# Opening of a hybrid decoder layer: norm 1's shift and scale by pairs of feature tiles on VectorE, the opening's order in a table, the causal mask in VectorE's maximum, keys flipped once

## The chip, the cores and the metric

The kernel runs on one core of one Trainium2 chip. The metric is the device time of one execution in microseconds (us). Engines by their names in the profile: PE is TensorE's matmul, PEld its weight load, DVE is VectorE, ACT is ScalarE, POOL is GpSimd, SP is SyncE, which issues nearly all transfers.

## What is computed

One decoder layer on 512 tokens of 1024 features, float32. Reduced to what matters here:

```python
sh1, sc1, gt1, sh2, sc2, gt2 = split(silu(c) @ w_ada + b_ada)      # 6 x 1024
h = rmsnorm(x, norm1_g) * (1.0 + sc1) + sh1
z = h @ w_in                      # HGRN2 q, f, i, g; NSA q; 6 key/value parts; gates
o_hg = hgrn2(hq, hf, hi, hgt, lb, hg_norm_g)        # 4 heads of 128, gated recurrence
q = rope(rmsnorm(nq)); k_c, k_s, k_w = rope(rmsnorm(kc)), ...   # 8 heads of 64, 2 key heads
# three attention branches: compressed keys, selected blocks, window; each a causal softmax
x = x + gt1 * (concat(o_hg, o_nsa) @ w_out)
h2 = rmsnorm(x, norm2_g) * (1.0 + sc2) + sh2
a, v = split(causal_dwconv(h2 @ w_up))
x = x + gt2 * ((silu(a) * v) @ w_down)
```

## The kernel before

Every large product is taken with both factors split into a high part (rounded by a cast) and a low part (the difference): `split` (L139 to L141) casts on ScalarE and subtracts on VectorE, and `mm3` (L143 to L146) does three products of 512 columns, high x high, high x low, low x high. The features are eight tiles of 128 (k = 0 to 7); the tokens are four tiles of 128.

**The opening.** x is loaded, normed and transposed into `xnT` (eight tiles of 128 x 512). For each feature tile k the shift and the scale are `silu(c) @ w_ada` for 2 x 128 columns; their 1 MB of w_ada comes in four transfers of 256 KB (L282, tiles `ada`), whose contiguous runs are 128 floats. The 1024 x 256 product is made in one of two ways. `ada_first_row` (L378) does it on TensorE: 8 products of 256 columns on each of the four row groups, one after another, into `warm`, copied to `row` on ScalarE. It is used for k = 0, 1 and those in `ROWS` (2, 3, 5). `ada_sum` (L392) does it on VectorE for k = 4, 6, 7 (`SUMS`): one multiplication (L401) and seven multiply-and-add steps (L399) of 128 x 256, into `rows`. `ada_col` (L406) turns the row into two columns by two tiny products `adc` (L411). `h_scale` (L414) makes shift and scale from them; `h_tile` (L429) has ScalarE scale the tile (L439) and cast it (L440), and VectorE subtract (L445) for the low part. The loop over k then does 18 products of 512 columns per tile: four token tiles of the NSA queries (`accq`) and two column tiles of the first forget gates (`accf`). The query weights of a tile (`raw`, 256 KB) and the gate weights of two tiles (`rawf`, 256 KB) are split as they come. `COLS` places `ada_col` and `h_tile` of tile k+1 between the products of tile k. GpSimd only makes powers for the norms and the rope tables (L485 to L527) in this part.

**Behind the opening.** A string `ORDER` interleaves generators letter by letter: `d` the dense projections, `p` the preparation of queries and keys, `a` attention, `s` the later sums of w_ada on VectorE (L1333, L1335), `l` and `m` the recurrence. The preparation of one unit (queries q0 to q3; keys k0 to k3; compressed keys a0 to a3) has four steps: `s` squares, `r` the root (GpSimd's power, L357), `n` norm and rope (L693 to L702), `f` the transposes (L751 queries, L797 keys, L838 compressed keys and values). For keys each head's 64 columns are written twice next to each other (`dup` = 2), so that one transpose gives them on partitions 0 to 63 and 64 to 127. In `scores` two key branches are handled together for the first two token tiles (n = 2): the causal mask is added by one more product of 256 columns (`identb` x `causb`, L981), and VectorE takes the maximum (L982). For the last two token tiles (n = 1) VectorE adds the mask `cmask` and takes the maximum in one instruction, with the result read by a second (L978).

Each engine does its instructions in the order in which the program gives them, and waits where an operand isn't ready.

## Time and profile before

| what | value |
|---|---|
| median of three runs | 699.65 us (699.53 to 701.13) |
| the profiled execution | 699.39 us |
| its span | 697.6 us |
| granted TensorE clock, mean | 1.00 |
| bytes moved | 90.16 MB, 129 GB/s over the span |

A row of a timeline gives the start, the length, the engine, the line, the operation, output<-inputs by the program's names, the shape, and how often it is repeated; in brackets stands the idle time ahead of it and what ended it. A row of groups gives busy time and mean nanoseconds of one. A row of waits gives the waiting engine and line, what it waited for, the sum, the times and the longest.

### The profile page before, as it was taken

What the parts mean: (1) busy time and instruction counts of PE and PEld (TensorE: products, weight loads), DVE (VectorE), ACT (ScalarE), POOL (GpSimd) and SP (SyncE); (2) the same over time, 40 slices, a digit from 0 to 9 for tenths busy, and PEclk for the clock granted to TensorE, in tenths of its full rate; (3) what the DMA queues carried; (4) which work ended last, traced back from release to release, by engine and by line L of the source; (5) the groups of instructions that cost most, each with busy time, mean ns of one, the idle gap of its engine ahead of it and who ended that gap; (6) DMA issues with size and microseconds to landing.
All of it is one profiled execution on the core that took longest, in us unless ns stands there. A gap on an engine that the chain in (4) does not pass through costs nothing.

```text
span 697.6 us, 10902 instructions
## 1 busy us (share of the span) xinstructions
PE 687.0 (98%) x4263; PEld 566.5 (81%) x4264; DVE 453.2 (65%) x882; ACT 326.0 (47%) x624; POOL 117.5 (17%) x119
## 2 busy tenths in 40 slices
PE   8999999999999999999999999999999999999997
PEld 4678898787887879888988888888888888888886
DVE  5588989968889879688656666655555554225224
ACT  5564446665676778245444443344433443111210
POOL 2005022200020200100047437511011010000000
PEclk9999999999999999999999999999999999999999
DMA  9996443568213226162053454523424323124301
GB/s 284 295 291 196 124 148 97 187 205 272 92 33 121 62 62 214 59 178 69 12 163 117 132 152 122 150 71 110 121 61 120 96 86 122 62 101 170 120 31 60
DMA packets 100487, 90.16 MB, mean 129 GB/s; under 512 B 5787, under 2 KB 83539, under 8 KB 100437
## 3 DMA queue, kind: packets, MB, share of 16 engines
q1 hardware_dynamic: 100181, 89.38, 42.0%
q8 instruction: 33, 0.54, 0.3%
q10 hardware_dynamic: 256, 0.11, 0.1%
q14 instruction: 17, 0.14, 0.1%
HBM read 87.37 MB, written 2.11 MB: 128 GB/s over the span
## 4 chain that ended last, share of the span: by engine, by line
PE 77%; DVE 10%; ACT 5%; DMA 4%; SPq 2%; issue 1%; POOL 0%; ACTq 0%; DVEq 0%
PE u L146 11%; PE u L144 11%; PE u L145 11%; PE dn L144 6%; PE dn L145 6%; PE dn L146 6%; PE pT L144 2%; PE pT L146 2%; PE pT L145 2%; PE oT L1059 2%; PE F L1031 2%; PE oh L144 2%; PE oh L146 2%; PE oh L145 2%; DMA raw<-in_w_in 1%; DVE rows L399 1%
## 5 line engine op out<-in xcount | busy, mean ns | idle before, releaser
L141 DVE TENSOR_TENSOR wlo<-raw,whi 128x1024 fp32r<-128x1024 f32 (+1 forms) x87 | 111.3, 1280 | 136.1 <-ACT whi L140 135.5
L140 ACT CAST whi<-raw 128x1024 fp32r<-128x1024 f32 (+1 forms) x87 | 89.8, 1032 | 102.3 <-PE dn L146 80.1
L144 PE MATMUL u<-h2h,whi 128*128 128x512 f32 (+1 forms) x360 | 136.7, 380 | 0.0
L145 PE MATMUL u<-h2l,whi 128*128 128x512 f32 (+1 forms) x360 | 136.7, 380 | 0.0
L146 PE MATMUL u<-h2h,wlo 128*128 128x512 f32 (+1 forms) x360 | 136.6, 380 | 0.0
L145 PEld LDWEIGHTS u<-h2l,whi 128*128 128x128 f32 x360 | 67.7, 188 | 12.9
L146 PEld LDWEIGHTS u<-h2h,wlo 128*128 128x128 f32 x360 | 67.7, 188 | 12.8
L144 PEld LDWEIGHTS u<-h2h,whi 128*128 128x128 f32 x360 | 67.7, 188 | 12.7
L145 PE MATMUL dn<-wlo,gT 128*128 128x512 f32 (+1 forms) x160 | 62.1, 388 | 0.0
L146 PE MATMUL dn<-whi,gT 128*128 128x512 f32 (+1 forms) x160 | 62.1, 388 | 0.0
L144 PE MATMUL dn<-whi,gT 128*128 128x512 f32 (+1 forms) x160 | 62.0, 388 | 0.0
L1623 POOL TENSOR_TENSOR y<-y,y 128x512 f32<-128x512 f32 x22 | 28.4, 1290 | 165.7 <-DVE y L1618 165.7
L140 ACT CAST gT<-y 128x512 fp32r<-128x512 f32 x20 | 12.4, 622 | 71.2 <-POOL y L1623 71.2
L141 DVE TENSOR_TENSOR gT<-y,gT 128x512 fp32r<-128x512 f32 x20 | 14.8, 742 | 42.7 <-ACT gT L140 42.7
L144 PE MATMUL pT<-hT,whi 128*128 128x512 f32 x96 | 39.2, 409 | 0.0
L146 PE MATMUL pT<-hT,wlo 128*128 128x512 f32 x96 | 37.7, 393 | 0.0
L145 PE MATMUL pT<-hT,whi 128*128 128x512 f32 x96 | 37.5, 391 | 0.0
L1621 ACT ACTIVATE y<-y 128x512 f32<-128x512 f32 x22 | 13.9, 632 | 49.6 <-DVE y L1618 49.6
L145 PEld LDWEIGHTS dn<-wlo,gT 128*128 128x128 f32 x160 | 30.0, 188 | 6.4 <-DVE wlo L141 0.2
L144 PEld LDWEIGHTS dn<-whi,gT 128*128 128x128 f32 x160 | 30.0, 188 | 6.2
L146 PEld LDWEIGHTS dn<-whi,gT 128*128 128x128 f32 x160 | 30.0, 188 | 6.2
L1616 ACT ACTIVATE y<-u,cv 128x512 f32<-128x512 f32 x44 | 33.9, 772 | 0.0
(378 smaller groups left out, 1410.2 us busy)
## 6 DMA issues: line engine op xcount, KB each, us to landing
raw<-in_w_up SPq DMA_DIRECT2D x44, 512.0 KB, 4.2
aw<-in_w_ada SPq DMA_DIRECT2D x24, 512.0 KB, 4.0
raw<-in_w_down SPq DMA_DIRECT2D x10, 1024.0 KB, 5.1
ada<-in_w_ada SPq DMA_DIRECT2D x32, 256.0 KB, 5.7
raw<-in_w_in SPq DMA_DIRECT2D x7, 1024.0 KB, 6.6
x<-in_x SPq DMA_DIRECT2D x8, 512.0 KB, 4.8
raw<-in_w_cmp SPq DMA_DIRECT2D x8, 512.0 KB, 5.6
raw<-in_w_out SPq DMA_DIRECT2D x4, 1024.0 KB, 6.1
```

The lines of the kernel that those rows point to most:

```text
L140: sc.copy(hi, src)
L141: (eng or ve).tensor_tensor(lo, src, f32(hi), ALU.subtract)
L144: pe.matmul(o, ah, bh, start=start, stop=False, skip_group_check=True)
L145: pe.matmul(o, ah, bl, start=False, stop=False, skip_group_check=True)
L146: pe.matmul(o, al, bh, start=False, stop=stop, skip_group_check=True)
L399: ve.scalar_tensor_tensor(t, w, cs[:, j:j + 1], t, ALU.mult, ALU.add)
L1031: pe.transpose(ps[:, j * P:(j + 1) * P], src[:, j * P:(j + 1) * P], ident)
L1059: pe.matmul(oTs[i][r:r + 64, h // 2], VV[:, j, b, g], src[:, q * P:(q + 1) * P], start=(h == 0 and b == 0 and j == 0), stop=False, skip_gr ...
L1616: sc.activation(y, u, AF.Identity, bias=cv[:, 132 + c:133 + c], scale=cv[:, 88 + c:89 + c])
L1621: sc.activation(y, y, AF.Silu)
L1623: gp.tensor_tensor(ys[0], ys[0], y, ALU.mult)
```

## The change

1. `GROUPS`: the feature tiles are handled as (0,), (1,), (2,3), (4,5), (6,7). Pairs are loaded by 256-column pieces (contiguous runs twice as long, 512 KB in a tile of two), and VectorE sums all three pairs, in 8 steps of 128 x 512 (L605, L607). TensorE makes rows for tiles 0 and 1 only.
2. The opening is written out by the table `OPEN`, one letter a step: `d` loads (their order in `LOADS`), `R` rows, `s` a step of a sum, `c` columns, `h` shift, scale and the high part, `l` or `g` the low part on VectorE or on GpSimd, `w` or `v` the query weights likewise, `f` or `e` the gate weights, `P` a part of the products. Twelve subtractions of 128 x 512 are thereby on GpSimd (4 of h, 5 of query weights, 3 of gate weights). The products of a tile go by kind (high x high for four token tiles, then high x low, then low x high).
3. ScalarE makes high part and scaled tile by two activations in place of an activation and a cast.
4. The rope tables, the first preparation steps and the forget gates are letters of `ORDER`, behind the opening.
5. The mask product is gone; every unit's mask and maximum are VectorE's combined instruction, for n = 2 once for each half.
6. Keys and compressed keys are no longer doubled: half as many transposes. ScalarE and VectorE write the two partition halves, and GpSimd copies one half of the high part (L861). The rope addition (L702) goes to GpSimd (L761).

```diff
-ROWS = (2, 3, 5)
-COLS = (0, 0, 1, 1, 2, 1, 2, 2)
-SUMS = {3: (4, 4, 4), 5: (6, 5, 3), 6: (7, 5, 3)}
-QUICK = 7
+GROUPS = ((0,), (1,), (2, 3), (4, 5), (6, 7))
+LOADS = "aqfaqmaqfqaqfqaqfqci"
+PROWS = (0, 1)
+OPEN = ("cvsshdPsPslRsPPsevPsddsdPsPPchgPdhsdPsdPsvvPgPPePPPsscPhsgPdsPPPhsvgsPssPPesshfPhllcwPPPPwtPP",)
...
     def load_ada():
-        k = len(ada)
+        ks = GROUPS[len(ada)]
+        c, per = len(ks) * P, 4 // len(ks)
         r = []
-        for half in range(2):
-            t = G([4, 2, P], s="ada")
+        for j in range(0, KT, per):
+            t = G([per, 2, c], s="ada")
             for e in range(2):
-                sp.dma_start(t[:, :, e], ada_first[:, 4 * half:4 * half + 4, e, k * P:(k + 1) * P])
-            r.append(t)
+                sp.dma_start(t[:, :, e], ada_first[:, j:j + per, e, ks[0] * P:ks[0] * P + c])
+            r += [t[:, a] for a in range(per)]
...
+    def sums_first():
+        for g in range(len(GROUPS)):
+            if g in PROWS:
+                continue
+            need("a", g + 1)
+            t = TMP([P, 2, len(GROUPS[g]) * P], tag="rows")
+            for j in range(KT):
+                if j:
+                    ve.scalar_tensor_tensor(t, ada[g][j], cs[:, j:j + 1], t, ALU.mult, ALU.add)
+                else:
+                    ve.tensor_scalar(t, ada[g][j], cs[:, 0:1], None, ALU.mult)
+                if j == KT - 1:
+                    arow[g] = t, ones[:, 0:1]
+                yield
...
+            for o in (h[:, 0], xk):
+                sc.activation(o, xk, AF.Identity, bias=sh1[:, k:k + 1], scale=a1[:, k:k + 1])
...
+            (gp if last["l"] == "g" else ve).tensor_tensor(hT[k][:, 1], xnT[k // 2][:, k % 2], f32(hT[k][:, 0]),
+                                                           ALU.subtract)
...
+            qw.append(first_weights(k, gp if last["w"] == "v" else None))
...
+            fw.append(first_gates(k, gp if last["f"] == "e" else None))
...
-            ve.tensor_tensor(dst[:, a, :, :, 0:16], dst[:, a, :, :, 0:16],
+            gp.tensor_tensor(dst[:, a, :, :, 0:16], dst[:, a, :, :, 0:16],
                              rt[:, a].unsqueeze(2).to_broadcast([P, g, dup, 16]), ALU.add)
...
         def flip_k(n):
             ps = PS()
+            for b in range(2):
+                pe.transpose(ps[:, b * P:(b + 1) * P], n[2][:, b].rearrange("p g a e -> p (g a e)"), ident)
+            ends = slice(0, 64), slice(64, 128)
             for g in range(2):
-                for b in range(2):
-                    pe.transpose(ps[:, (2 * g + b) * P:(2 * g + b + 1) * P],
-                                 kd[:, b, g].rearrange("p a e -> p (a e)"), ident)
-            for g in range(2):
-                split(KK[g, 0][:, i], KK[g, 1][:, i],
-                      ps[:, g * 256:g * 256 + 256].rearrange("p (b n) -> p b n", b=2))
+                pv = ps[ends[g], 0:256].rearrange("p (b n) -> p b n", b=2)
+                sc.copy(KK[g, 0][ends[g], i], pv)
+                gp.tensor_copy(KK[g, 0][ends[1 - g], i], KK[g, 0][ends[g], i])
+                for r in range(2):
+                    ve.tensor_tensor(KK[g, 1][ends[r], i], pv, f32(KK[g, 0][ends[g], i]), ALU.subtract)
...
-        if n == 1:
-            pt = TMP([P, 512], tag="pt")
-            ve.tensor_tensor_reduce(pt[:, 0:W], ps[:, 0:W], cmask[:, 512 - W:512], -1.0, 1e30, ALU.add, ALU.min,
-                                    mx[:, 0:1])
-            return pt, mx
-        pe.matmul(o[:, i], identb, causb.unsqueeze(1).to_broadcast([P, n, P]), start=False, stop=True)
-        ve.tensor_reduce(mx[:, 0:n], ps[:, 0:n * W].rearrange("p (b w) -> p b w", b=n), AX.X, ALU.max,
-                         negate=True)
-        return ps, mx
+        pt = TMP([P, 512], tag="pt")
+        for e in range(n):
+            ve.tensor_tensor_reduce(pt[:, e * W:(e + 1) * W], ps[:, e * W:(e + 1) * W], cmask[:, 512 - W:512], -1.0,
+                                    1e30, ALU.add, ALU.min, mx[:, e:e + 1])
+        return pt, mx
```

How the table moves instructions, first on VectorE, in the later part of the opening. In the kernel before, `rows` are the sums (L401, L399), L415 and L416 are shift and scale, L445 is the low part of a tile and L141 that of weights:

```order
L141 TENSOR_TENSOR wq_72_551<-raw_52_372,wq_72_551 128x512
L415 TENSOR_TENSOR sh1_178<-adc_27_199,vt_169 128x1
L416 SCALAR_TENSOR_TENSOR a1_177<-adc_27_199,bsc1_170,vt_169 128x1
L401 TENSOR_SCALAR rows_74_564<-ada_64_485,cs_141 128x256
L399 SCALAR_TENSOR_TENSOR rows_74_564<-ada_64_485,cs_141,rows_74_564 128x256 x3
L399 SCALAR_TENSOR_TENSOR rows_74_564<-ada_65_488,cs_141,rows_74_564 128x256
L445 TENSOR_TENSOR hT_73_561<-xnT_18_175,hT_73_561 128x512
L399 SCALAR_TENSOR_TENSOR rows_74_564<-ada_65_488,cs_141,rows_74_564 128x256 x3
L141 TENSOR_TENSOR wq_76_593<-raw_52_372,wq_76_593 128x512
```

Now, from the end of the sum of tiles 2 and 3 (`rows_49`) on; `rows_58` is the sum of tiles 4 and 5, from four tiles `ada_53` to `ada_56`, and the two shifts and scales (L425, L426) behind its first step are those of tiles 2 and 3:

```order
L605 SCALAR_TENSOR_TENSOR rows_49_328<-ada_48_325,cs_133,rows_49_328 128x512 x2
L607 TENSOR_SCALAR rows_58_388<-ada_53_369,cs_133 128x512
L425 TENSOR_TENSOR sh1_170<-adc_25_189,vt_161 128x1
L426 SCALAR_TENSOR_TENSOR a1_169<-adc_25_189,bsc1_162,vt_161 128x1
L425 TENSOR_TENSOR sh1_170<-adc_25_189,vt_161 128x1
L426 SCALAR_TENSOR_TENSOR a1_169<-adc_25_189,bsc1_162,vt_161 128x1
L605 SCALAR_TENSOR_TENSOR rows_58_388<-ada_53_369,cs_133,rows_58_388 128x512
L605 SCALAR_TENSOR_TENSOR rows_58_388<-ada_54_372,cs_133,rows_58_388 128x512 x2
```

The sums are now twice as wide, the subtractions are gone from between them, and the shift and scale of a pair stand behind the first step of the next pair's sum. On GpSimd, in the kernel before, the rows behind the four powers of norm 1 are the rope tables:

```order
L485 TENSOR_SCALAR hgg_121<-hgg_121 128x1
L486 TENSOR_SCALAR gains_120<-gains_120 128x64
L525 TENSOR_TENSOR ctab_20_190<-gains_120,co_189 128x16x8
L526 TENSOR_TENSOR stab_191<-gains_120,sn_188 128x16x8
L525 TENSOR_TENSOR ctab_20_190<-gains_120,co_189 128x16x8
```

Now at the same place stand the twelve subtractions (L141 of weights, L633 of tiles):

```order
L141 TENSOR_TENSOR wq_44_309<-raw_7_103,wq_44_309 128x512
L141 TENSOR_TENSOR wf_51_358<-rawf_8_105,wf_51_358 128x512
L141 TENSOR_TENSOR wq_52_361<-raw_7_103,wq_52_361 128x512
L633 TENSOR_TENSOR hT_59_404<-xnT_15_166,hT_59_404 128x512
L141 TENSOR_TENSOR wq_66_440<-raw_7_103,wq_66_440 128x512
L141 TENSOR_TENSOR wq_67_443<-raw_57_382,wq_67_443 128x512
L633 TENSOR_TENSOR hT_61_415<-xnT_15_166,hT_61_415 128x512
L141 TENSOR_TENSOR wf_68_458<-rawf_60_411,wf_68_458 128x512
L633 TENSOR_TENSOR hT_69_487<-xnT_16_167,hT_69_487 128x512
L141 TENSOR_TENSOR wq_72_515<-raw_57_382,wq_72_515 128x512
L633 TENSOR_TENSOR hT_71_511<-xnT_16_167,hT_71_511 128x512
L141 TENSOR_TENSOR wf_73_533<-rawf_60_411,wf_73_533 128x512
```

Behind them come the mask's table, the rope tables, the powers of all four query units, and then the first rope addition (L761). On TensorE the columns of tiles 6 and 7 (L422) now stand between the products of tile 4 and those of tile 5, where each tile's columns stood inside the products of the tile ahead of it.

More of the change, by code (lines that the diff above doesn't have):

```diff
@@ L255, in next_parts @@
         w = ahead.pop(0)
-        if more:
+        begun.append(1)
+        if more and not ahead:
             piece()
         return w
-    crow = cst.tile([8, P], F32, name="crow")
-    sp.dma_start(crow, d["c"].rearrange("b (k p) -> (b k) p", p=P))
     cb = cst.tile([P, C_COLS], F32, name="cb")
@@ L318, in load_small, with load_consts, load_more, need @@
         sp.dma_start(hgg, d["hg_norm_g"].rearrange("b e -> e b"))
+    def load_consts():
+        sp.dma_start(cb[:, C_LMASK:], d["consts"][:, C_LMASK:])
+    def load_more():
+        n = sum(loaded.values())
+        if n == len(LOADS):
+            return False
+        letter = LOADS[n]
+        {"a": load_ada, "q": load_q, "f": load_f, "m": load_small, "c": load_consts, "i": issue}[letter]()
+        loaded[letter] += 1
+        return True
+    def need(letter, n):
+        while loaded[letter] < n:
+            assert load_more()
+    loaded = dict.fromkeys("aqfmci", 0)
+    for _ in range(5):
+        load_more()
     ones = cst.tile([P, P], F32, name="ones")
@@ L640, in hybrid_layer_kernel @@
-        if n < KT:
-            w, wfk = wn, wfn
+                    pe.matmul(accq[i], h[:, e, i * P:(i + 1) * P], w[:, f], start=(k + e + f == 0),
+                              stop=(e == 1 and k == KT - 1), skip_group_check=True)
+                yield
+            if k > 1:
+                reach("f", k // 2)
+            w = fw[k // 2]
+            for j in range(2):
+                sl = slice(j * P, (j + 1) * P)
+                mm3(accf[j], w[:, 0, k % 2, sl], w[:, 1, k % 2, sl], h[:, 0], h[:, 1], k == 0, k == KT - 1)
+                yield
@@ new lines, in piece_first, with advance @@
+    def piece_first():
+        need("i", 1)
+        for _ in range(2):
+            if not begun:
+                piece()
+            yield
+    opening = {"P": products_first(), "R": rows_first(), "s": sums_first(), "c": columns_first(), "h": high_first(),
+               "l": low_first(), "w": weights_first(), "f": gates_first(), "d": loads_first(), "t": tables,
+               "k": piece_first()}
+    same = {"g": "l", "v": "w", "e": "f"}
+    made = dict.fromkeys(opening, 0)
+    def advance(letter):
+        name = same.get(letter, letter)
+        last[name] = letter
+        if next(opening[name], opening) is opening:
+            return False
+        made[name] += 1
+        return True
@@ L644, in proj_tok, with reach @@
+    def reach(name, n):
+        while made[name] < n:
+            assert advance(name), name
+    for row in OPEN:
+        for letter in row:
+            advance(letter)
+    for name in "dsRchwflP":
+        while advance(name):
+            pass
     def proj_tok(res, more=True):
@@ L1474, in hybrid_layer_kernel @@
                   proj_T(hg_gate_out(1), False), late())
-    streams = {"d": dense, "p": prep(PREP), "a": attention(adas), "c": cmp_out(), "s": ada_sums(),
-               "l": hg_levels(0, As[0]), "m": hg_levels(1, As[1])}
+    streams = {"d": dense, "p": prep(PREP), "a": attention(adas), "c": cmp_out(), "s": sums_later(),
+               "l": hg_levels(0, As[0]), "m": hg_levels(1, As[1]), "F": forget_first(), "t": tables, "k": opening["k"]}
     for row in ORDER:
         for step in row:
-            next(streams[step], None)
+            if step in "tk":
+                advance(step)
+            else:
+                next(streams[step], None)
+    for name in "tk":
+        while advance(name):
+            pass
     for g in streams.values():
```

253 lines of the change are left out of this document (115 added, 138 removed).

## The prediction

> **What bounds it now.** I read the page's first lines first, then the table of stretches, then the timeline of TensorE at the seam between the opening and the stage behind it.
>
> ```profile
> span 697.6 us, 10902 instructions
> PE 687.0 (98%) x4263; PEld 566.5 (81%) x4264; DVE 453.2 (65%) x882; ACT 326.0 (47%) x624; POOL 117.5 (17%) x119
> PE 77%; DVE 10%; ACT 5%; DMA 4%; SPq 2%; issue 1%; POOL 0%; ACTq 0%; DVEq 0%
> ```
>
> TensorE is busy 98% of the span and carries 77% of the chain that ends last. So outside the opening an edit counts by what it takes from TensorE or makes TensorE wait. The stretches show where VectorE has room. In the next view each row is a stretch: its length, then the busy time of TensorE, its weight loads, VectorE, ScalarE and GpSimd, the granted clock, the DMA share and GB/s.
>
> ```profile
> 16.20:60.90 44.70, 42.69 (x238) 31.11 (x238) 32.17 (x87) 25.18 (x44) 5.30 (x11) 1.00 0.98 279
> 60.90:110.00 49.10, 48.59 (x273) 42.15 (x271) 44.52 (x103) 21.53 (x43) 12.26 (x10) 1.00 0.49 151
> 110.00:180.00 70.00, 69.40 (x722) 56.11 (x720) 58.91 (x139) 43.21 (x132) 7.51 (x10) 1.00 0.55 174
> ```
>
> The first row is the opening from its first product. TensorE idles 2.0 us there, and the DMA share is 0.98: TensorE and the transfers end nearly together. GpSimd works 5.3 us of 44.7. In the two later stretches TensorE idles 0.5 and 0.6 us, so what is taken from TensorE there is gained almost whole; VectorE idles 4.6 and 11.1 us.
>
> ```profile
> 56.80 0.39 PE L144 MATMUL accq<-wq,hT 128*128 128x512 f32 x1
> 60.88 0.39 PE L144 MATMUL kva<-whi,hT 128*128 128x512 f32 x1
> ```
>
> These are the first product of the last feature tile and the first of the next stage: 18 products in 4.08 us, 0.227 each. The opening ends at 60.88.
>
> **The opening: who pays for the sums.** Three pair sums now stand on VectorE (L605, L607), 8 steps of 512 elements each, where three sums of 8 steps of 256 stood; twelve 512-wide subtractions go to GpSimd. Prices:
>
> ```profile
> L399 DVE SCALAR_TENSOR_TENSOR rows<-ada,cs,rows x21: 477/485/486, 32.8 to 52.9; 128x256 f32<-128x256 f32 x21
> L401 DVE TENSOR_SCALAR rows<-ada,cs x3: 342/342/347, 32.4 to 49.0; 128x256 f32<-128x256 f32 x3
> L1333 DVE SCALAR_TENSOR_TENSOR aacc<-aw,cs,aacc x21: 1270/1279/1286, 72.8 to 271.7; 128x1024 f32<-128x1024 f32 x21
> L1335 DVE TENSOR_SCALAR aacc<-aw,cs x3: 746/748/749, 69.4 to 220.8; 128x1024 f32<-128x1024 f32 x3
> L141 DVE TENSOR_TENSOR wq<-raw,wq 128x512 fp32r<-128x512 f32 x7 | 4.8, 688 | 3.5 <-ACT wq L140 3.5
> 364.93 1.29 POOL L1623 TENSOR_TENSOR y<-y,y 128x512 f32<-128x512 f32 x1 [0.44 <-DVE y L1618]
> ```
>
> Between 256 and 1024 elements, an even slope puts a 512-wide step at 0.75 us (I use 0.765, allowing for the fixed part) and the first at 0.48: a pair costs 0.48 + 7 x 0.765 = 5.8 us. A 512-wide subtraction is 0.69 on VectorE and 1.29 on GpSimd, by the nearest two-input row (L1623). If the engines were independent, GpSimd would have room. The rows where both work say otherwise:
>
> ```profile
> 367.30 1.62 POOL L1407 TENSOR_TENSOR aw<-aw 128x512 f32<-128x512 f32 x1
> 366.91 0.85 DVE L141 TENSOR_TENSOR gT<-y,gT 128x512 fp32r<-128x512 f32 x1 [2.12 <-ACT gT L140]
> 367.86 2.14 DVE L141 TENSOR_TENSOR wlo<-raw,whi 128x1024 fp32r<-128x1024 f32 x1
> 56.55 1.23 POOL L525 TENSOR_TENSOR ctab<-gains,co 128x128 f32<-128x128 f32 x1 [29.51 <-DVE co L517]
> 57.73 0.46 POOL L526 TENSOR_TENSOR stab<-gains,sn 128x128 f32<-128x128 f32 x1
> 56.23 1.23 DVE L141 TENSOR_TENSOR wlo<-raw,whi 128x1024 fp32r<-128x1024 f32 x1
> ```
>
> At 367 both are stretched: GpSimd 1.62 instead of 1.29, VectorE's subtraction of 1024 elements 2.14 instead of 1.23. At 56.55 GpSimd's 128-element step takes 1.23, until VectorE's long one ends at 57.46, and the like step behind it 0.46. So a VectorE operation with two inputs in SBUF and a GpSimd operation take turns; one turn overlaps the next by some 0.14 us: VectorE's first ends at 367.76, GpSimd's 1.16 later for work of 1.29, VectorE's second 1.08 after that for work of 1.23. Every step of a sum (two inputs in SBUF) and every moved subtraction is such an operation.
>
> [...]
>
> When does this queue begin? The transfers of the pairs have 1 KB packets in place of 512 bytes:
>
> ```profile
> ada<-in_w_ada SPq DMA_DIRECT2D x32, 256.0 KB, 5.7
> raw<-in_w_in SPq DMA_DIRECT2D x8, 256.0 KB, 5.2
> 29.98 0.64 PE L385 MATMUL warm<-ada,cs 128*32 128x256 f32 x8 [0.78 <-DMA ada<-in_w_ada]
> 35.00:37.00 2.00, 1.81 (x9) 1.20 (x7) 1.89 (x5) 1.02 (x2) 0.00 (x0) 1.00 1.18 292
> 48.00:50.00 2.00, 2.00 (x11) 1.70 (x11) 1.93 (x7) 0.89 (x2) 0.00 (x0) 1.00 1.06 390
> ```
>
> Before, TensorE waits until 29.98 for the fourth tile's piece of w_ada; in the queue up to and with it stand 4 MB of w_ada and 1.25 MB of weights (the five pieces like the second row's, 256 KB each by their shapes). Now pair (2,3) is complete after 4.75 MB: 0.5 MB less, 1.8 us at 292 GB/s (the stretch of 512-byte packets). The 390 GB/s stretch moves 2 KB packets; I estimate 350 between the two for the pairs, 1.2 us less for 2 MB. So (2,3) lands near 26.9 and its sum ends near 29.5. Three weight pieces (0.75 MB) and the first 512 KB of pair (4,5) then land near 31.5 (30.4 at 390 and 350, 32.6 if all of it goes at 292). VectorE's order puts the first step of pair (4,5) ahead of the shift and scale of tiles 2 and 3: those wait for it, and behind them ScalarE, the subtractions and TensorE. So the queue starts at 31.5.
>
> From then on stand two pair sums and ten of GpSimd's twelve subtractions (two stand ahead): 2 x 5.8 + 10 x 1.29 = 24.6 us, less 0.14 for each of some 20 turns, 21.8; with the overlap on every operation it would be 21.2. I take 22: the last sum ends at 53.5 (51.6 to 57.2 by the ends of both). The four column products of pair (6,7) follow, and TensorE's order has them directly ahead of feature tile 5's products.
>
> ```profile
> 53.48 0.61 PE L411 MATMUL adc<-ones,rows 128*128 128x1 f32 x4 [0.23 <-DVE rows L399]
> ```
>
> Four pieces of a column product take 0.5 to 0.6 here for one tile; I allow 0.8 for the pair. Then 54 products: 54 x 0.227 = 12.3. The opening ends at 53.5 + 0.8 + 12.3 = 66.6, against 60.88: **+5.7 us** (+3.8 to +9.4). If three of the ten subtractions came only after the last sum, it would be +2.2.
>
> **Keys, values, mask.** TensorE loses 16 mask products and 16 transposes:
>
> ```profile
> 113.14 0.28 PE L981 MATMUL S<-causb,identb 128*128 128x256 bf16 x1
> 113.26 0.38 PE L838 MATMUL ps<-cb,dst 128*128 128x128 f32 x2
> 96.40 0.60 PE L797 MATMUL ps<-cb,dst 128*128 128x128 f32 x4
> 96.76 0.38 PE L144 MATMUL acca<-whi,hT 128*128 128x280 f32 x1
> ```
>
> From start to start 0.12 us for one mask product, 0.36 for four transposes: 16 x 0.12 + 4 x 0.36 = **-3.3 us**, and since TensorE idles 1.1 us in these 119 us nearly all of it counts; I take **-3.2**. VectorE gets the mask:
>
> ```profile
> L982 DVE TENSOR_REDUCE mx<-S 128x2 f32<-128x512 f32 x8 | 5.4, 683 | 0.0
> L982 DVE TENSOR_REDUCE mx<-S 128x2 f32<-128x256 f32 x8 | 3.7, 464 | 0.0
> L978 DVE CUSTOM_DVE_ANT_0 pt<-S,cmask 128x512 f32<-128x512 f32 x16 | 11.0, 686 | 0.1
> L978 DVE CUSTOM_DVE_ANT_0 pt<-S,cmask 128x384 f32<-128x384 f32 x16 | 8.7, 552 | 0.2 <-PE S L974 0.2
> L978 DVE DVE_READ_ACCUMULATOR2_ANT mx<- 128x1 f32 x32 | 2.7, 83 | 0.0
> ```
>
> By the slope between 384 and 512 a masked maximum over 256 costs 0.42 and over 128 0.28, and 0.08 more to read the result: 16 x 0.50 + 16 x 0.36 = 13.8 in place of 9.1, +4.7 us. Against it stand sixteen rope additions that leave VectorE and key products that are half as wide, while the keys' low parts become twice as many. What covers the mask is the 11.1 us that VectorE idles in its stretch; I charge +0.3 for waits (0, if the cover holds throughout, to 1.5, if a third of the mask's 4.7 falls where TensorE has nothing else).
>
> GpSimd now adds the rope term (L761) ahead of the queries' transposes, and in its order the powers for all four query units, and the rope tables, stand ahead of the first addition.
>
> ```profile
> PE ps L751 <- DVE dst L702: 0.5, 1, 0.5
> 60.33 3.30 POOL L357 TENSOR_TENSOR hrs<-hrs,mhalf 128x8 f32<-128x8 f32 x2
> ```
>
> TensorE already waits 0.5 us for the first of these; one power takes 1.65. I take +0.4 (0 to 1.65).
>
> **Sum.** Against the profiled run's own time, 699.39 (span 697.6 and 1.8 around it; the median of the three runs is 699.65): 699.39 + 5.7 + 0.4 - 3.2 + 0.3 = **702.6 us**. 0.3%, or 2.1 us, is about what a measurement of this kernel can tell from no change.
>
> **Rivals.** (A) The engines do not exclude each other for these operations: faster. Then the chain from pair (2,3) decides. One of its links, ScalarE's scaling of a tile, is in the trace:
>
> ```profile
> 32.52 0.81 ACT L439 ACTIVATE xnT<-xnT,sh,a 128x512 f32<-128x512 f32 x1 [0.96 <-DVE a L416]
> ```
>
> The chain: its sum at 29.5, 0.6 for the columns, 0.4 that I allow for shift and scale, 0.81 on ScalarE and 1.29 on GpSimd give the first product of tile 2 at 32.6, and 108 products later it is 57.1; with 0.6 + 0.6 for two more pairs' columns and 0.7 of waits, 59.0, or -1.9: 699.39 - 1.9 + 0.4 - 3.2 + 0.3 = 695.0.
>
> For it: no row shows precisely a 512-wide step of this kind beside a 512-wide GpSimd subtraction. Against it: the six rows above. Chance 0.23.
>
> (B) The exclusion holds, but VectorE's queued steps win the turns, and the subtractions fall between the sums. Then the sums wait only for transfers and the late subtractions hold up single tiles: the opening ends near 63, +2.1, and the total is 699.0. The rows at 367 show turns, which is against it. Chance 0.10.
>
> (C) As forecast, and TensorE's clock falls. Half of the queue frees the columns of (4,5), near 42.4; 0.8 for these, 0.4 for shift and scale, 0.81 on ScalarE and 1.29 on GpSimd later come tile 4's products, 45.7 to 49.8. TensorE then stands for some 3.7 us until 53.5.
>
> ```profile
> 1.59 3.55 PE L326 MATMUL warm<-wrm 128*128 128x512 bf16 x8 [1.59 <-DVE mhalf L328]
> 7.09 1.89 PE L346 MATMUL warm<-wrm 128*128 128x512 bf16 x8
> ```
>
> The first eight products of the program take 3.55 us, the same eight later 1.89: a cold start costs 1.7 us, which makes 704.3. No later stall in this trace is that long, so the rows don't say whether one resets the clock; I take a wait as long as that first stretch, 3.55 us, as the point from which it decides, and 3.7 is just above it. [...] Chance 0.12, with the cases in which VectorE has no room behind the opening.
>
> The forecast keeps 0.55; by its own bounds (opening +2.2 to +9.4) it falls within 0.3% in 0.13 of that and is slower in 0.42. Slower: 0.42 + 0.12 = 0.54; within 0.3%: 0.13 and most of B, 0.20; faster: A and the rest of B, 0.26. The range goes from A's 695.0 to 707.0, the forecast with the opening at +9.4 (706.3) and 0.7 for the rope term between its ends.
>
> **What would show it.** Right, if the mean of L605 is well above 0.77 us and GpSimd's L141 and L633 above 1.29; if TensorE's waits name the columns (L422) for VectorE's rows, with 2 us and more each; if the first kva product starts near 66.6; and if TensorE then runs from there to the end 2.5 us faster than before. A mean of L605 at 0.77 with kva at 59 is rival A; a low granted clock in the stretch behind the stall is C; a wait at the queries' transposes over 1 us makes the rope term wrong. If kva starts before 62, the step that fails is the queue of 22 us on the shared path.

## The result: slower by 1.3%

The changed kernel takes 708.73 us (median of 4 runs, 708.62 to 709.57), the kernel before 699.59 (4 runs, 699.28 to 701.13): ratio 1.0129, 95% interval 1.0111 to 1.0146. That is +9.1 us where +3.2 was forecast, and outside the stated range. The profiled execution has 709.57, its span is 707.8 (before 697.6, +10.2). The page of the changed kernel begins:

```profile
span 707.8 us, 10810 instructions
PE 686.9 (97%) x4184; PEld 567.4 (80%) x4184; DVE 458.2 (65%) x901; ACT 328.3 (46%) x630; POOL 146.7 (21%) x153
PE 69%; DVE 15%; ACT 6%; DMA 5%; issue 2%; SPq 2%; POOL 1%; DVEq 0%; ACTq 0%; POOLq 0%
```

TensorE's share of the chain that ended last fell from 77 to 69%, VectorE's rose from 10 to 15%. The three stretches that the prediction showed, now:

```profile
16.20:60.90 44.70, 35.62 (x157) 27.35 (x157) 32.25 (x54) 19.74 (x35) 19.91 (x16) 0.89 0.82 266
60.90:110.00 49.10, 48.02 (x264) 41.32 (x263) 42.46 (x96) 22.90 (x41) 22.96 (x27) 1.00 0.43 131
110.00:180.00 70.00, 66.61 (x609) 52.26 (x607) 57.35 (x171) 43.88 (x136) 11.81 (x22) 0.98 0.58 186
```

In the first TensorE idles 9.1 us (before 2.0), GpSimd works 19.9 (5.3), and the granted clock is 0.89. Two stretches at half make this mean: 20.5 to 23.9 us, behind waits of 1.1 and 0.5 us between 17.2 and 19.4, and 51.2 us onwards. In the third TensorE idles 3.4 us (0.6) at a clock of 0.98.

**The opening.** TensorE's timeline from the last product of tile 4 on:

```profile
48.69 0.39 PE L146 MATMUL accf<-hT,wf 128*128 128x512 f32 x1
52.50 1.87 PE L422 MATMUL adc<-ones,rows 128*128 128x1 f32 x8 [3.42 <-DVE rows L605]
54.23 4.77 PE L657 MATMUL accq<-wq,hT 128*128 128x512 f32 x12
60.21 2.88 PE L657 MATMUL accq<-wq,hT 128*128 128x512 f32 x12
68.37 0.39 PE L144 MATMUL kva<-whi,hT 128*128 128x512 f32 x1
```

TensorE stands for 3.4 us until the last sum is there. The columns then take 1.73 us from start to start, and tile 5's products 5.98 (54.23 to 60.21) where a tile takes 4.08 at full rate. The next stage begins at 68.37, 7.5 us later than before. The clock in short stretches (the first number behind the last bracket, 1.00 or 0.50):

```profile
50.00:51.00 1.00, 0.00 (x0) 0.00 (x0) 0.96 (x2) 0.00 (x0) 1.00 (x2) 1.00 0.31 123
51.50:52.50 1.00, 0.00 (x1) 0.00 (x1) 0.94 (x1) 0.00 (x0) 1.00 (x3) 0.50 0.01 4
55.00:57.00 2.00, 2.00 (x7) 1.52 (x6) 0.58 (x1) 1.97 (x3) 0.00 (x0) 0.50 0.00 0
59.00:60.00 1.00, 1.00 (x6) 0.79 (x6) 1.00 (x4) 0.38 (x2) 0.00 (x0) 1.00 0.00 0
```

The clock falls to half during the stand, at 51.2, and comes back at 58.1, 5.6 us after the columns began. The earlier stretch at half, to 23.9, does not show in the end of the opening: behind it the queue on VectorE begins with a transfer, at 30.84. What TensorE waited for, on VectorE and on GpSimd:

```profile
30.84 1.23 DVE L607 TENSOR_SCALAR rows<-ada,cs 128x512 f32<-128x512 f32 x1 [1.43 <-DMA ada<-in_w_ada]
32.37 9.08 DVE L605 SCALAR_TENSOR_TENSOR rows<-ada,cs,rows 128x512 f32<-128x512 f32 x7
44.18 8.27 DVE L605 SCALAR_TENSOR_TENSOR rows<-ada,cs,rows 128x512 f32<-128x512 f32 x6
```

```profile
29.25 1.28 POOL L141 TENSOR_TENSOR wf<-rawf,wf 128x512 fp32r<-128x512 f32 x1 [8.02 <-ACT wf L140]
36.10 3.12 POOL L141 TENSOR_TENSOR wq<-raw,wq 128x512 fp32r<-128x512 f32 x2 [0.27 <-ACT wq L140]
48.52 1.71 POOL L633 TENSOR_TENSOR hT<-xnT,hT 128x512 fp32r<-128x512 f32 x1
50.19 1.71 POOL L141 TENSOR_TENSOR wf<-rawf,wf 128x512 fp32r<-128x512 f32 x1
```

The turns are as forecast: a step of a sum takes 1.30 and 1.38 us on average (9.08 / 7 and 8.27 / 6), a subtraction 1.71 where one alone, the first row, takes 1.28, and the queue runs from 30.84 to 52.45, 21.6 us. The first step, L607, has only one tile as input, and it is stretched too: 1.23 us beside a subtraction, where the same step of the next sum, with none beside it, takes 0.48.

**Behind the opening.** The last lines of two tables of stretches, from the start of the `kva` stage to the end (kernel before, then changed):

```profile
sum 636.72, PE 630.59 PEld 528.11 DVE 412.92 ACT 291.68 POOL 108.74; mean PE 126.12 PEld 105.62 DVE 82.58 ACT 58.34 POOL 21.75
```

```profile
sum 639.43, PE 629.46 PEld 526.22 DVE 411.61 ACT 293.73 POOL 121.11; mean PE 125.89 PEld 105.24 DVE 82.32 ACT 58.75 POOL 24.22
```

This part is 2.7 us longer, where the forecast had 2.5 less. TensorE idles 10.0 us in it instead of 6.1, and its busy time falls by 1.1 only, though 3.3 us of work are gone; a second stretch at half clock, of 3.4 us, explains up to 1.7 of that. The largest new waits of TensorE from 60 to 300 us in the changed kernel (for the queries' transposes, L812, it had waited 0.5 us for VectorE):

```profile
PE F L1084 <- DVE pt L1075: 1.6, 1, 1.6
PE ps L812 <- POOL dst L761: 0.9, 1, 0.9
PE pT L144 <- ACT kv L900: 0.8, 1, 0.8
```

The largest stands at 144.5 to 146, and the half clock follows it, from 146.8 to 150.2:

```profile
144.50:146.00 1.50, 0.00 (x0) 0.00 (x0) 1.43 (x9) 0.81 (x5) 0.00 (x0) 1.00 0.51 74
147.00:149.50 2.50, 2.50 (x24) 1.57 (x16) 2.33 (x9) 1.71 (x8) 0.00 (x0) 0.50 1.08 384
```

VectorE's timeline ahead of it has the masked maximum (L1036), for which ScalarE and then TensorE wait, behind the additions for the compressed keys, which take turns with the same additions on GpSimd. These turns are not new (3.63 us in the kernel before, from 129.21); there TensorE waited 0.2 us at this place:

```profile
138.61 3.58 DVE L933 TENSOR_TENSOR flat<-kv,pet 128x248 f32<-128x248 f32 x4
142.44 1.37 DVE L141 TENSOR_TENSOR wlo<-raw,whi 128x1024 fp32r<-128x1024 f32 x1
143.74 1.21 DVE L1218 TENSOR_TENSOR hgQ<-hgQ,hgT 128x1024 f32<-128x1024 f32 x1
144.87 0.28 DVE L1036 CUSTOM_DVE_ANT_0 pt<-S,cmask 128x128 f32<-128x128 f32 x1
```

### The profile page after: what moved, and what is told of

The parts are those of the page before. It is cut to its first block, busy times and chain, and to the rows that moved or that the text cites. A ratio compares the mean times of both kernels' runs of the same rounds, so it can differ in the third digit from the quotient of the medians.

```text
span 707.8 us, 10810 instructions
## 1 busy us (share of the span) xinstructions
PE 686.9 (97%) x4184; PEld 567.4 (80%) x4184; DVE 458.2 (65%) x901; ACT 328.3 (46%) x630; POOL 146.7 (21%) x153
## 4 chain that ended last, share of the span: by engine, by line
PE 69%; DVE 15%; ACT 6%; DMA 5%; issue 2%; SPq 2%; POOL 1%; DVEq 0%; ACTq 0%; POOLq 0%
PE u L145 11%; PE u L146 11%; PE u L144 11%; PE dn L145 6%; PE dn L144 6%; PE dn L146 6%; DMA raw<-in_w_in 3%; DVE wlo L141 2%; DMA ada<-in_w_ada 2%; PE oh L144 2%; PE oh L146 2%; PE oh L145 2%; DVE aacc L1386 2%; PE oT L1112 1%; PE F L1084 1%
## 5 line engine op out<-in xcount | busy, mean ns | idle before, releaser
L141 DVE TENSOR_TENSOR wlo<-raw,whi 128x1024 fp32r<-128x1024 f32 (+1 forms) x87 | 110.2, 1267 | 135.4 <-ACT whi L140 134.9
L144 PE MATMUL u<-h2h,whi 128*128 128x512 f32 (+1 forms) x360 | 136.7, 380 | 0.0
L145 PE MATMUL u<-h2l,whi 128*128 128x512 f32 (+1 forms) x360 | 136.7, 380 | 0.0
L146 PE MATMUL u<-h2h,wlo 128*128 128x512 f32 (+1 forms) x360 | 136.7, 380 | 0.0
L1052 ACT ACTIVATE pt<-pt,mx 128x128 f32<-128x128 f32 (+3 forms) x64 | 35.9, 562 | 22.6 <-DVE mx L1036 21.5
L141 DVE TENSOR_TENSOR gT<-y,gT 128x512 fp32r<-128x512 f32 x20 | 14.8, 742 | 43.6 <-ACT gT L140 43.6
```

Source lines behind the costliest of these rows:

```text
L141: (eng or ve).tensor_tensor(lo, src, f32(hi), ALU.subtract)
L144: pe.matmul(o, ah, bh, start=start, stop=False, skip_group_check=True)
L145: pe.matmul(o, ah, bl, start=False, stop=False, skip_group_check=True)
L146: pe.matmul(o, al, bh, start=False, stop=stop, skip_group_check=True)
L1052: sc.activation(pt[:, sl], pt[:, sl], AF.Exp, bias=mx[:, e:e + 1], scale=-1.0, accum_out=su[:, h % 2, e:e + 1])
```

## Experiments

Theory T: GpSimd's subtractions and VectorE's sums take turns, and this sets the opening's end. Theory V: behind the opening the saving on TensorE turns into waits for VectorE and GpSimd. The rivals stand with each run. In the table "next stage" is the start of the `kva` products in the profiled run, "behind" its span less that. The medians of the kernel before beside them were 698.9 to 699.6. A profiled run is one execution of several, so "next stage" and "behind" can differ from what the medians say by the spread between executions.

| run | median us | ratio to before | 95% interval | next stage | behind |
|---|---|---|---|---|---|
| kernel before | 699.59 | 1 | | 60.88 | 636.7 |
| changed kernel | 708.73 | 1.0129 | 1.0111 to 1.0146 | 68.37 | 639.4 |
| e1_subs_on_vector | 715.45 | 1.0231 | 1.0217 to 1.0245 | 74.63 | 639.0 |
| e2_filler | 708.54 | 1.0135 | 1.0119 to 1.0150 | 66.93 | 639.4 |
| e5_no_subtractions | 701.21 | 1.0027 | 1.0018 to 1.0037 | 60.58 | 639.3 |
| e8_table | 704.05 | 1.0069 | 1.0056 to 1.0082 | 59.65 | 641.2 |
| e9_table_old_parts | 704.28 | 1.0078 | 1.0066 to 1.0091 | 61.26 | 641.3 |
| e10_table_copied_rope | 702.23 | 1.0046 | 1.0032 to 1.0059 | 62.41 | 639.3 |
| e6_opening_only | 708.79 | 1.0138 | 1.0122 to 1.0153 | 67.46 | 638.1 |
| e3_mask_on_tensor | 709.87 | 1.0147 | 1.0133 to 1.0161 | 67.85 | 639.2 |
| h1_before_attention | 702.60 | 1.0044 | 1.0031 to 1.0056 | 61.29 | 639.5 |
| h2_before_flips | 702.78 | 1.0049 | 1.0037 to 1.0062 | 60.58 | 640.1 |
| h3_before_mask | 699.80 | 1.0006 | 0.9998 to 1.0015 | 60.82 | 637.1 |
| h6_before_compressed | 699.04 | 0.9999 | 0.9990 to 1.0008 | 61.04 | 636.7 |
| h7_before_flips_copied | 699.65 | 1.0008 | 0.9999 to 1.0017 | 62.10 | 637.0 |
| c1_before_compressed_mask | 698.92 | 1.0003 | 0.9994 to 1.0012 | 61.53 | 636.6 |

### The subtractions on VectorE, at the same places

```diff
-OPEN = ("cvsshdPsPslRsPPsevPsddsdPsPPchgPdhsdPdsPvvPgPPePPPsscPhsgPdsPPPhsvgsPssPPesshfPhllcwPPPPwtPP",)
+OPEN = ("cwsshdPsPslRsPPsfwPsddsdPsPPchlPdhsdPdsPwwPlPPfPPPsscPhslPdsPPPhswlsPssPPfsshfPhllcwPPPPwtPP",)
```

> The changed kernel with its twelve opening subtractions on VectorE again; the sums, the loads and the rest stay. Theory T (a sum's step and a GpSimd subtraction take turns on a path that both share, and this sets the opening's end): the steps of the sums go back from a mean above 1 us to 0.75, VectorE alone has two sums of 5.7 and ten subtractions of 0.69 from 30.8 on, 18.3 us, so the last sum ends near 50 and the next stage starts near 63.5 to 65 in place of 68.4; total 704 to 705.5. Rival R (VectorE has too much to do with three wide sums, and GpSimd takes work off it): VectorE gets 12 x 0.69 = 8.3 us more, the next stage starts after 70, total 711 or more.

715.45 us: theory T's number is missed by 10 us, and rival R's is met. But its reason isn't what the trace shows. The sums are short again, and VectorE stands in line for ScalarE:

```profile
L605 DVE SCALAR_TENSOR_TENSOR rows<-ada,cs,rows x21: 741/752/752, 22.5 to 57.1; 128x512 f32<-128x512 f32 x21
35.89 0.69 DVE L633 TENSOR_TENSOR hT<-xnT,hT 128x512 fp32r<-128x512 f32 x1 [1.73 <-ACT xnT L626]
48.50 0.69 DVE L633 TENSOR_TENSOR hT<-xnT,hT 128x512 fp32r<-128x512 f32 x1 [1.34 <-ACT xnT L626]
52.29 0.69 DVE L141 TENSOR_TENSOR wq<-raw,wq 128x512 fp32r<-128x512 f32 x1 [1.58 <-ACT wq L140]
```

The median step is 0.752, the longest too. What the expectation left out: at these places of the table a subtraction comes right behind its shift and scale, ScalarE needs 1.7 us in between, and on VectorE the sum's next step waits behind it; on GpSimd only GpSimd waits. TensorE then stands 5.0 us for the last sum, and behind it the columns take 1.72 us and the next twelve products 5.27 (59.65 to 64.92), where the twelve ahead of the stand take 2.72 (48.68 to 51.40); the granted clock of the run is 0.983. This run changes two things at once and doesn't decide; the next one and e8 do.

### Without the subtractions

```diff
-            (gp if last["l"] == "g" else ve).tensor_tensor(hT[k][:, 1], xnT[k // 2][:, k % 2], f32(hT[k][:, 0]),
-                                                           ALU.subtract)
+            if last["l"] == "g":
+                gp.memset(f32(hT[k][:, 1]), 0.0)
...
+        if eng:
+            sc.copy(w[:, 0], raw_q[k])
+            eng.memset(f32(w[:, 1]), 0.0)
+            return w
```

> The changed kernel with GpSimd's twelve subtractions left out: it writes zeros into the low parts instead, which reads nothing in SBUF (about 0.53 us each by the memset of the same size), so these low parts are missing from the result. Everything else, the order on VectorE too, stays. Theory T (the turns with GpSimd's reading operations stretch the sums): the sums' steps have a mean of 0.75, the last sum ends near 45, 1.5 us behind the last piece of w_ada (near 43), TensorE no longer stands for over 3 us, the clock stays, and the next stage starts near 59 to 60.5 in place of 68.4; total 700 to 703. Rival R (three wide sums are too much for VectorE, or TensorE's order makes the stand): steps or not, the last sum ends near 50 and the next stage starts at 64 or later.

701.21 us, next stage at 60.58: theory T. VectorE's order is the same, and the same two rows of the sums are now

```profile
31.98 5.47 DVE L613 SCALAR_TENSOR_TENSOR rows<-ada,cs,rows 128x512 f32<-128x512 f32 x7
42.32 4.68 DVE L613 SCALAR_TENSOR_TENSOR rows<-ada,cs,rows 128x512 f32<-128x512 f32 x6
```

0.78 us a step in place of 1.30 and 1.38; the last sum ends at 47.0, 5.5 us earlier (rival R had 50), and from there on TensorE runs at full rate (a product every 0.23 us): columns and 54 products take 13.5 us in place of 15.9. The two make the 7.8 us by which the next stage comes earlier. "The clock stays" was too much: from 31.1 to about 34.5, ahead of the stand's place, the products come at about half the pace (0.42 to 0.43 us apart), and the granted clock of the run is 0.993. Nine of the memsets are done before 18.2 us, since they wait for no cast, so the sums of the queue have no GpSimd operation beside them at all. The other three stand beside VectorE's operations with two inputs in SBUF, and neither side is stretched:

```profile
24.84 0.53 POOL L520 MEMSET wq<- 128x512 f32 x1 [6.66 <-PE accq L667]
25.31 0.53 POOL L642 MEMSET hT<- 128x512 f32 x1
```

```profile
24.66 1.54 DVE L613 SCALAR_TENSOR_TENSOR rows<-ada,cs,rows 128x512 f32<-128x512 f32 x2 [1.87 <-DMA ada<-in_w_ada]
26.11 0.69 DVE L644 TENSOR_TENSOR hT<-xnT,hT 128x512 fp32r<-128x512 f32 x1
```

### TensorE kept busy while it stands

```diff
+            if g == len(GROUPS) - 1:
+                warm_up(12)
             ada_cols(g)
```

> The changed kernel with 12 products of 512 columns into an unused buffer ahead of the columns of tiles 6 and 7, in the time in which TensorE stands there (3.4 us); 12 x 0.236 = 2.8 us. Theory T (that stand lets TensorE's clock fall to half, and the columns and the first products of tile 5 pay for it: 1.73 us instead of 0.8 and 14.1 instead of 12.3): the granted clock stays at 1.00 there, the next stage starts near 65.6, total 705.9. Rival R (the slow columns and products have another cause, the stand itself being the whole loss): nothing changes, 708.7, or it gets later by what the filling pushes back.

At this place the mechanism is as expected; its price isn't found in the time (705.9 was expected). In the profiled run the columns and the products are at full rate:

```profile
53.51 0.95 PE L422 MATMUL adc<-ones,rows 128*128 128x1 f32 x8
66.93 0.39 PE L144 MATMUL kva<-whi,hT 128*128 128x512 f32 x1
```

From the columns to the next stage it is 13.42 us in place of 15.87, 2.45 less. But the columns began 1.0 us later in this run, for two reasons. The last sum ended 0.4 later (52.89), as its queue began later. And tile 4's products came at about half the pace (0.42 to 0.43 us apart in place of 0.23) from 43.9 to about 47.3, where the changed kernel's clock is at 1.00; the filling began only at 51.13 and was itself in the columns' way for 0.6. So 1.4 us of the 2.45 are left at the next stage, and the profiled executions differ by as much (708.12 and 709.57); the medians are 708.54 and 708.73, with ranges that overlap. That a stand without products lets the clock fall here is borne out by the filling, in one profile, and by the slow products behind e1's longer stand (5.27 us for twelve); what its removal is worth in the total stays open between 0 and 2.5 us.

### Another table: VectorE alone, with steps of the next sum between scale and subtraction

```diff
-OPEN = ("cvsshdPsPslRsPPsevPsddsdPsPPchgPdhsdPdsPvvPgPPePPPsscPhsgPdsPPPhsvgsPssPPesshfPhllcwPPPPwtPP",)
+OPEN = ("cwsshdPsPslRsPPsPsddsdPPPPPcfwhhdsslPPsslwPPPddssssPPPcfwhhssPPlPPPdsslwPPssssPPPcfwhhPPlPPPwlPPPPPtPP",)
```

> The changed kernel with another table for the opening and nothing else: all twelve subtractions on VectorE, none of GpSimd's, and two or more steps of the next sum between a pair's shift and scale and its subtractions, so that VectorE doesn't wait for ScalarE. Theory T (the turns with GpSimd lose the opening; that VectorE alone was slower still in the first such run came from its waits for ScalarE in order): two sums 11.4 and ten subtractions 6.2 from 31 on, the last sum ends near 48.5, TensorE runs on, the next stage starts near 60 to 61.5; behind it 639.3 as in the changed kernel: total 701 to 703. Rival R (VectorE can't carry three wide sums and the subtractions): the next stage starts after 65, total 706 or more.

Next stage at 59.65, within theory T's 60 to 61.5 or better, against 68.37 with GpSimd's help: VectorE alone carries the sums and the subtractions. The time is above the expected 701 to 703 and gains less than the 8.7 us of the opening: 7.0 us between the profiled executions, by the ratios 0.6% or 4.2 us (1.0069 against 1.0129). The two profiled executions are the fastest of this kernel's five and the slowest of the changed kernel's four, so the gap between 7.0 and 4.2 is spread between runs. In its profile TensorE stands at the head of the next stage, in two waits that the later start had covered:

```profile
PE kva L144 <- ACT tmp L793: 1.7, 1, 1.7
PE kva L145 <- DVE wlo L141: 0.7, 1, 0.7
```

The first is the forget gates, which the new order has behind the opening; the second is the low part of the first weights of the stage.

### Behind the opening: the parts on the kernel before

The masked maximum, the keys flipped once and the rope addition on GpSimd are put into the kernel before with its own order (their lines are those of the change). The runs with flipped keys also take over the change's form of the rope product, one instruction for each part of a unit in place of one for each half of the 16 columns:

> The kernel before with the parts of the change that lie behind the opening and nothing else: masked maximum on VectorE, keys flipped once, rope addition on GpSimd; its opening and its order stay. Prediction's term (TensorE's 3.2 us less count almost whole, 0.7 comes back as waits): 697.1. Rival V (VectorE is late there already, so the saving turns into waits for VectorE or GpSimd): 699 to 702.

702.60, +3.0 us where the forecast's terms make -2.5: the error behind the opening shows without the opening. Next, the parts one by one. First the flips (h2; the lines are those of the keys, the compressed keys have the like edit):

```diff
-                for b in range(2):
-                    pe.transpose(ps[:, (2 * g + b) * P:(2 * g + b + 1) * P],
-                                 kd[:, b, g].rearrange("p a e -> p (a e)"), ident)
+            for b in range(2):
+                pe.transpose(ps[:, b * P:(b + 1) * P], n[2][:, b].rearrange("p g a e -> p (g a e)"), ident)
...
```

> The kernel before with only the keys and compressed keys flipped once (16 transposes less on TensorE, 1.3 us; GpSimd copies half of the high parts; VectorE writes 16 half subtractions in place of 8); rope addition on VectorE, mask on TensorE. If TensorE bounds: 698.3. If VectorE or GpSimd's copies are late: 700 to 701.5.

Then the mask (h3):

```diff
...
-        pe.matmul(o[:, i], identb, causb.unsqueeze(1).to_broadcast([P, n, P]), start=False, stop=True)
-        ve.tensor_reduce(mx[:, 0:n], ps[:, 0:n * W].rearrange("p (b w) -> p b w", b=n), AX.X, ALU.max,
-                         negate=True)
+        for e in range(n):
+            ve.tensor_tensor_reduce(pt[:, e * W:(e + 1) * W], ps[:, e * W:(e + 1) * W], cmask[:, 512 - W:512], -1.0,
+                                    1e30, ALU.add, ALU.min, mx[:, e:e + 1])
...
```

> The kernel before with only the masked maximum on VectorE (TensorE 1.9 us less, VectorE 4.7 more). If TensorE bounds: 697.7. If VectorE is late near 130 to 145, where its queue holds the flat additions, and the wait of 1.6 us for the scaled weights comes with this part alone: 700 to 702.

The flips alone cost 3.5 us; the mask alone is within what can be told from no change (1.0006, 0.9998 to 1.0015), so the 1.9 us that it takes from TensorE come back. They come back as two waits of TensorE, here with the mask and then in the kernel before:

```profile
PE F L1023 <- DVE pt L1014: 1.5, 1, 1.5
PE cps L885 <- DMA raw<-in_w_cmp: 1.0, 2, 0.8
```

```profile
PE cps L888 <- DMA raw<-in_w_cmp: 0.4, 1, 0.4
PE F L1031 <- ACT pt L1020: 0.2, 1, 0.2
```

The wait for the scaled weights F is 1.5 to 1.6 us in all three runs on the kernel before that have the mask (h1, h3, c1), and at most 0.5 in the three that don't (h2, h6, h7). Ahead of it VectorE has no gap to take the mask in, in the kernel before already: it is busy for 7.42 of 7.50 us, and TensorE for all of them.

```profile
129.20:136.70 7.50, 7.50 (x47) 5.48 (x45) 7.42 (x12) 3.62 (x13) 4.17 (x5) 1.00 0.06 16
```

With the flips (h2), the timeline of the last key unit on VectorE is

```profile
113.69 0.87 DVE L804 TENSOR_TENSOR KK<-ps,KK 64x256 fp32r<-64x256 f32 x2 [0.43 <-ACT KK L801]
```

The low parts of all key units, with the flips and then in the kernel before:

```profile
L804 DVE TENSOR_TENSOR KK<-ps,KK x16: 408/423/428, 96.9 to 114.1; 64x256 fp32r<-64x256 f32 x16
```

```profile
L141 DVE TENSOR_TENSOR KK<-ps,KK x8: 416/424/425, 97.4 to 111.3; 128x256 fp32r<-128x256 f32 x8
```

TensorE's wait for the last of them and the clock around it, with the flips again:

```profile
114.70 0.36 PE L972 MATMUL S<-KK,qs 128*128 128x256 f32 x1 [1.32 <-DVE KK L804]
114.00:116.00 2.00, 0.85 (x6) 0.67 (x6) 1.79 (x8) 0.92 (x5) 0.25 (x1) 1.00 0.00 0
116.00:118.00 2.00, 2.00 (x8) 1.54 (x7) 1.83 (x9) 1.95 (x7) 1.64 (x3) 0.54 0.00 0
```

The half subtractions cost as much as whole ones, there are twice as many, and the first scores wait 1.3 us for them; behind that wait the clock falls, to 0.54. The fall isn't what costs the 3.5 us: of the five timed runs with the flips the two with a granted clock of 0.999 and 1.000 are the slowest (702.96 and 703.20). Two runs test whether it is this chain; the first is shown against the run with the flips (h2):

```diff
-                for r in range(2):
-                    ve.tensor_tensor(KK[g, 1][ends[r], i], pv, f32(KK[g, 0][ends[g], i]), ALU.subtract)
+                ve.tensor_tensor(KK[g, 1][ends[g], i], pv, f32(KK[g, 0][ends[g], i]), ALU.subtract)
+                gp.tensor_copy(KK[g, 1][ends[1 - g], i], KK[g, 1][ends[g], i])
```

> The kernel before with all keys flipped once, but VectorE subtracts one half only and GpSimd copies the low half too (8 VectorE subtractions of 0.42 less, 8 GpSimd copies of 0.41 more); mask on TensorE, rope addition on VectorE. Theory K: VectorE's chain is as short as before, the first scores' wait of 1.3 us for the keys goes, and the half clock behind it: 698.5 to 700. Rival G (any late key does it, GpSimd's copies stand in the chain just as VectorE's subtractions did, or take turns with VectorE): 701 to 703.

> The kernel before with only the compressed keys and their values flipped once (8 transposes less on TensorE, 0.7 us; two copies more on ScalarE); the other keys stay doubled, mask on TensorE, rope addition on VectorE. Theory K (what costs 3.4 us when all keys are flipped once is the chain of the other keys: VectorE's four half subtractions of 0.42 a unit in place of two, in two pairs with ScalarE's cast between them): no loss here, 698.6 to 699.5. Rival C (the compressed keys' later copies make TensorE wait ahead of its transposes): 700.5 to 702.

699.65 and 699.04: both as theory K has it. With one subtraction fewer for each head the flips cost 0.7 us or nothing (1.0008, 0.9999 to 1.0017), and the compressed keys cost nothing; nor do they gain the 0.7 us.

> The kernel before with the mask on VectorE and the compressed keys flipped once, nothing else: TensorE has 2.6 us less. If TensorE bounds: 697. If VectorE's queue near 130 to 145 turns the saving into waits as with the mask alone: 699 to 700.5.

698.92 against 698.99: 2.6 us less work on TensorE, no difference.

### The parts, taken back from the changed kernel

```diff
...
+        pe.matmul(o[:, i], identb, causb.unsqueeze(1).to_broadcast([P, n, P]), start=False, stop=True)
+        ve.tensor_reduce(mx[:, 0:n], ps[:, 0:n * W].rearrange("p (b w) -> p b w", b=n), AX.X, ALU.max,
+                         negate=True)
...
```

> The changed kernel with the causal mask of the first two token tiles by a product on TensorE again (16 x 0.12 = 1.9 us of TensorE), VectorE taking only the maximum (4.7 us less). Theory V (behind the opening VectorE is what is late, and TensorE's saved time turns into waits): the wait of 1.6 us for the scaled weights near 146 goes, and with it the half clock that follows (1.8 us); total 707 or less. Rival P (TensorE is the bound there): the 1.9 us come on top, 710.6.

709.87: not the 707 of theory V, nearer to rival P's 710.6, and not told apart from the changed kernel (the intervals overlap). The wait for the scaled weights is still 1.4 us, so in the new order the mask isn't its cause by itself. Next, all three parts taken back (e6), the same with the rewritten table (e9), and the rewritten table with VectorE's rope addition and the copied keys (e10):

> The changed kernel with the parts behind the opening taken back: mask on TensorE, keys flipped twice, rope addition on VectorE; the new opening and the new order stay. If the loss of the opening (7.5 us at the start of the next stage) is carried to the end whole: 707. If the losses of the two parts simply add to 9.1 and the part behind the opening has the 3.0 that it had on the kernel before: 705.7. If the new order behind the opening makes its own waits: 708 or more.

> The same table, and behind the opening the kernel before's mask on TensorE, doubled keys and rope addition on VectorE, in the new order. If the parts behind the opening cost the 2.7 us there: 698 to 699.5. If the new order costs it, with or without these parts: 701 to 703, as with them.

> The same table with the new parts, but VectorE subtracts one half of the keys' low part and GpSimd copies it, and the rope addition is VectorE's again. If the keys' chain and GpSimd's rope addition are what costs behind the opening: 1.5 to 3 us less than with the table alone, 699 to 700.5. If it is VectorE's queue as a whole: no gain.

e6 has 708.79, as its third case has it and like the changed kernel with its 708.73; e9 has 704.28, above both of its ranges and like e8 with its 704.05. In the new order the three parts make no difference, and without them the part behind the opening is still longer than before: 638.1 and 641.3 against 636.7. Two waits of the new order can be named. Without the mask TensorE still waits 1.0 and 1.1 us for the scaled weights F (0.2 before), and in e9, as in e8, it stands 1.7 us for the forget gates and 0.7 for the low part of the weights at the head of the stage, 2.4 of the 4.6. e10 has 702.23: 1.8 us less than e8, as its first case has it, but not the 699 to 700.5 named with it, since e8 itself came out higher. The intervals of the two just overlap, and the keys' chain and the rope addition may have any share (e10's opening starts late in the profiled run: TensorE's first transposes waited 3.6 us for x, in the others 0.3 to 0.8). So two things lose time there, each of them shown without the other: the flips in the old order, and the new order without the flips (by e9's median, and by the profiled runs of e6 and e9, one each). Which of the order's moves does it (forget gates, rope tables, preparation steps) wasn't tried singly.

## Why the prediction was wrong

**The turns** ("two pair sums and ten of GpSimd's twelve subtractions", "I take 22"): right. The queue began at 30.84 (forecast 31.5) and took 21.6 us. That it came so near to 22 is partly luck: in it VectorE stands 1.15 us for the columns of tiles 4 and 5, which the forecast didn't count, and the work itself took 20.5. The waits named as a sign, "2 us and more each" for the columns, were 0.9, 1.25 and 3.4 us. Without the reading GpSimd operations the sums are at 0.78 a step (e5), and rival A, no exclusion, is out. A subtraction of 1.28 us alone takes 1.71 in turns with steps of 0.75 alone (e1), a little less than their sum of 2.03. Rival B fails by the same rows, both sides being stretched. Only the prediction's restriction to operations with two inputs was too narrow: the first step of a sum, with one tile as input, was stretched from 0.48 to 1.23 us.

**The end of the opening** ("53.5 + 0.8 + 12.3 = 66.6"): the first number was 52.45, the others came out as 1.73 and 14.14, and the end at 68.37. The term that was mis-sized is this tail, by 2.8 us: the half clock, rival C, which the prediction had with 0.12 and a price of 1.7. It is no rival but a consequence of the forecast's own stand: 3.4 us of it were enough, where the prediction wanted 3.55. In the profile the tail's 2.8 us, less the 1.0 by which the sum ended earlier than forecast, make the step from +5.7 to +7.5. In the timed runs the filling brought 0.2 (e2), with another slow stretch elsewhere in its profile (43.9 to about 47.3).

**Behind the opening** ("I take -3.2", "nearly all of it counts", "+0.3 for waits"): this step failed. The prediction read from TensorE's idle 1.1 us in 119 that what is taken from TensorE is gained. The same rows had VectorE busy for 103.4 of 119.1 us, and it is VectorE's chain, not its sum, that counts: what TensorE no longer does, it waits for. TensorE's work fell by 0.7 to 3.2 us in h3, h6, c1 and h1, and nothing was gained in any of them; 3.5 were lost where the keys' chain on VectorE grew (h2). The cover named for the mask, 11.1 us of idle VectorE in 70, is not at the place where it was needed: from 129.2 to 136.7 us VectorE was busy throughout, and the mask's 1.9 us came back as 1.3 more of the wait for F behind it and 0.6 more of a wait for weights (h3). The rope term (+0.4) fits: 0.9 us of wait in place of 0.5; no run has that part alone. (The sum 16 x 0.12 + 4 x 0.36 is 3.4, not 3.3.) What the new order does was left out of the sum altogether; e6 and e9 put it at 1.4 and 4.6 us behind the opening, by one profiled run each.

**The sum**: opening +7.5 and behind it +2.7 make the +10.2 of the profiled run (+9.1 in the medians), where +5.7 and -2.5 were forecast. The direction came from the turns and was right; of the 7.0 us that the forecast missed in the profile, 5.2 are the step behind the opening and 1.8 the opening's tail.

## What to carry to other kernels

An engine that is busy 98% of the time doesn't make its work the bound: ask which chain feeds the next instruction, and cost a halving of TensorE's work by what the feeding engine must then do, in that order. Work moved to GpSimd didn't relieve VectorE here, since the two took turns (1.30 and 1.38 us a step in place of 0.75, 1.71 a subtraction in place of 1.28); count both in one sum, and weigh it against VectorE's in-order waits for ScalarE, up to 1.7 us each in e1. When a forecast has TensorE standing for microseconds, put the half clock behind it into the sum: in the changed kernel's profile its stretches lasted 3.41, 6.83 and 3.41 us, so I estimate at most 1.7 us for each 3.41, half its length. And look at the spread before reading a difference between two profiles: those of e8 and the changed kernel differ by 7.0 us, their ratios by 4.2.
